# A planned order for the attention stage, seven products for the third group's queries and keys, and rotated rows by DMA

## The chip, the cores and the metric

The kernel runs on one core of one Trainium2 chip. The metric is the device time of one execution in microseconds (us). The core has five instruction streams that run beside each other and meet at semaphores: PE (TensorE, matmuls), DVE (VectorE), ACT (ScalarE), POOL (GpSimd) and SP (SyncE, which here issues nearly all loads from memory). PSUM holds the matmuls' sums in banks of 512 columns.

## What is computed

Two layers on 512 tokens of width 1024. Each layer has a mixer and a gated FFN; scale, shift and gate vectors come from a conditioning vector `c`. Layer 0's mixer is a recurrent one (hgrn), layer 1's is the attention that is changed here: three groups with windows and dilations, mixed by their log sums.

```python
DILATED_GROUPS = ((128, 1), (512, 4), (2048, 16))

def dilated_attention_mixer(u, cos, sin, w_in, w_out):
    proj = (u @ w_in).reshape(B, S, N_GROUPS, 3, ATT_HEADS, ATT_HEAD_DIM)
    for gi, (window, dilation) in enumerate(DILATED_GROUPS):
        q = apply_partial_rope(proj[:, :, gi, 0], cos, sin) * scale
        k = apply_partial_rope(proj[:, :, gi, 1], cos, sin)
        v = proj[:, :, gi, 2]
        o_g, lse_g = dilated_group_attention(q, k, v, window, dilation)
    wts = jax.nn.softmax(jnp.stack(lses, axis=0), axis=0)
    o = jnp.einsum('gbsh,gbshd->bshd', wts, jnp.stack(outs, axis=0))
    return o.reshape(B, S, D_MODEL) @ w_out

def reference(...):
    cond = jax.nn.silu(c)
    for layer in range(2):
        mod = cond @ ada_w[layer] + ada_b[layer]
        sh1, sc1, g1, sh2, sc2, g2 = jnp.split(mod, 6, axis=-1)
        u = rms_norm(h, norm_g[layer, 0]) * (1.0 + sc1) + sh1
        y = hgrn2_mixer(u, ...) if layer == 0 else dilated_attention_mixer(u, ...)
        h = h + (1.0 + g1) * rms_norm(y, norm_g[layer, 1])
        u = rms_norm(h, norm_g[layer, 2]) * (1.0 + sc2) + sh2
        h = h + (1.0 + g2) * rms_norm(swiglu_ffn(u, ...), norm_g[layer, 3])
```

The rotation (`apply_partial_rope`) touches the first 32 of a head's 128 dimensions. In the text "vector (l, v)" is the v-th of the six vectors of layer l, counted from 0: (1,4) is the second scale of layer 1.

## The kernel before

**Products in three parts.** Every float32 operand is cut into hi (a cast to the reduced type fp32r) and lo (the remainder), and every product is hi·hi + hi·lo + lo·hi on PE (`three`, L438 to L440 for most of them).

**The stream of weights.** All weights come through `Stream`, in one list of items. SP loads an item (1 MB, `_load`, L59 to L68) into one of two raw tiles; ACT casts hi (L88), DVE subtracts for lo (L89), and a raw tile is free for the next load when lo is done. There are three pairs of hi and lo tiles. `take()` hands out the next weight and casts up to two weights ahead of it (`ahead = parts - 1`), `take(0)` casts no further than the one that it hands out. Items of the conditioning vectors ("ada", `ada_chunk`) stand in the same list, put between weights by `weave`: a load of 1 MB, four sums on DVE (L257, L259), after every second one a reduction over partitions on POOL (L261), and then small sums with the identity on DVE (L271, L275).

**Seven products.** Some products are done as a block scheme: the weight is taken in quarters of 512 columns, and seven products of quarter sums replace eight. The first FFN's `seven_products` (matmuls at L853) does this with 84 matmuls of 128x256 where 96 would be needed; `seven_values` does it for the values of groups 1 and 2 of the attention.

**The attention stage.** `order` lists units: for each of eight heads and three groups one unit "qk" (queries and keys, a weight of 1 MB: 2 x 8 x 3 = 48 matmuls of 128x512 by `block`), and units "v" for values. After the two halves of a unit `qk_evac` (L1704, L1705) has ACT copy 32 rows to be rotated, and all 128 rows, out of PSUM; `turn_pair` (L1712 to L1715 on DVE) rotates the rows, and four copies on ACT (L1720, L1722) put them back. The rest of a head (scores, exponentials, weights of the groups, scaling of the probabilities in `merge_r` and `merge_n` on DVE (L1798, L1805), transposes `flip` with their copies on DVE (L1817) and ACT (L1815), sums with V) is given to `Fillers`, which runs it a fixed number of half units later. There is no planner: outside hand-ordered stretches (`manual_schedule`, which keeps the code's order on PE, ACT, DVE and POOL) the framework's scheduler sets the order of each engine.

**The seam.** Behind the last unit comes `mixer_out`, the product with `attn_w_out` (four weights), in the code's own order. It asks for its first weight with `take(0)` at kt = 0 and for the second at kt = 4; between its products stand the rest of heads 6 and 7 (`tail`). By then the stage's own `take()` calls have cast two weights ahead. `cut(kt)` makes hi and lo of the attention's output (`oh`, `ol`).

Of the kernel before, what the change touches and what calls it, by code (L numbers as in the profile page):

```python
# [1 line left out]

# [13 lines left out]
P = 128  # L16
# [21 lines left out]
class Stream:  # L38
# [73 lines left out]
    def whole(self):  # L112

        assert self.items[self.done][0] in WHOLE
        self.fill()
        self.done += 1
        return self.raw.pop(self.done - 1)
# [10 lines left out]
    def take(self, ahead=None):  # L128
        ahead = self.parts - 1 if ahead is None else ahead
        k = min(self.taken + ahead, len(self.wpos) - 1)  # L130
        stop = next((i for i in range(self.done, len(self.items)) if self.items[i][0] in WHOLE), len(self.items))
        self.process_to(min(self.wpos[k] + 1, stop))
        if k == len(self.wpos) - 1:
            self.process_to(stop)
        self.taken += 1
        return self.ready.pop(0)

# [21 lines left out]
def block_kernel(tc, x, c, positions, ada_w, ada_b, norm_g, hgrn_w_in, lower, hgrn_norm_g, hgrn_w_out,  # L159
# [8 lines left out]
    with ExitStack() as ctx:  # L168
# [95 lines left out]
        def ada_item(l, v, hf, kq):  # L264
            src = ada_w[l, kq * 512:(kq + 1) * 512, v * D + hf * 512:v * D + (hf + 1) * 512]
            return ("ada", src.rearrange("(k p) n -> p k n", p=P), ada_chunk(l, v, hf, kq))
# [43 lines left out]
        def fin_item(l, v, hf):  # L310
            if v not in (2, 5):
                return ("do", None, col_fin(l, v, hf))
# [3 lines left out]
            return ("rows", (b, n), row_fin(l, v, hf))  # L316
# [62 lines left out]
        items += weave(f0b[:9], ada_seq((1, 1), (1, 0)), 0, 0.9) + f0b[9:]  # L379
# [31 lines left out]
        late = ada_seq((1, 2), (1, 4), (1, 3))  # L411
# [3 lines left out]
        woven(late[:8], 1.5)  # L415
# [4 lines left out]
        woven(late[8:], 1.3)  # L420
# [16 lines left out]
        def three(ps, ah, al, bh, bl, start, stop):  # L437
            pe.matmul(ps, ah, bh, start=start, stop=False)  # L438
            pe.matmul(ps, ah, bl, start=False, stop=False)  # L439
            pe.matmul(ps, al, bh, start=False, stop=stop)  # L440
# [942 lines left out]
        def seven_values(dsts, apart, th, tl):  # L1383


            C = lambda raw, c: V4(raw)[:, :, c * 256:c * 256 + 256]
            G = lambda t, o: V4(t[:, o * 1024:(o + 1) * 1024])
            u_of = lambda r, c: lambda kt, n: [a[:, r * 4 + kt, c * 256 + n * P:c * 256 + (n + 1) * P] for a in apart]
            t_of = lambda i: lambda kt, n: [a[:, i, kt, n * P:(n + 1) * P] for a in (th, tl)]
            raws, tiles = {}, {}  # L1390

            def cut(i, tile, o, k, c):
                hi, lo = tiles[i, tile]
                src = C(raws[i][k], c)
                act.copy(G(hi, o), src)
                dve.tensor_sub(G(lo, o), src, G(hi, o).bitcast(F32))

            def place(i, tile):
                tiles[i, tile] = st.part_tiles(V0)

            def prepare(i, step):
                if i >= len(dsts):
                    return
                if step == 0:
                    raws[i] = [st.whole(), st.whole()]
                    place(i, 0)
                    cut(i, 0, 0, 0, 0)
                    cut(i, 0, 1, 1, 1)
                elif step == 1:
                    place(i, 1)  # L1410
                    cut(i, 1, 0, 1, 0)
                    a, b = raws[i]
                    dve.tensor_add(C(b, 1), C(b, 1), C(a, 1))
                    dve.tensor_add(C(a, 1), C(a, 1), C(a, 0))
                    dve.tensor_add(C(a, 0), C(a, 0), C(b, 1))
                    dve.tensor_add(C(b, 0), C(b, 0), C(a, 0))
                    cut(i, 1, 1, 0, 0)
                elif step == 2:
                    place(i, 2)
                    cut(i, 2, 1, 0, 1)  # L1420
                    st.fill(1)
                    cut(i, 2, 0, 1, 1)
                else:
                    place(i, 3)
                    cut(i, 3, 0, 1, 0)
                    raws.pop(i)
                    st.fill()

            def run(ps, i, tile, o, us):
                hi, lo = tiles[i, tile]  # L1430
                for n in range(2):
                    for kt in range(4):
                        w = slice(o * 1024 + kt * 256, o * 1024 + (kt + 1) * 256)
                        three(ps[:, n * 256:(n + 1) * 256], *us(kt, n), hi[:, w], lo[:, w], kt == 0, kt == 3)

            H2 = lambda a: a.rearrange("p (n c) -> p n c", n=2)
            for step in range(3):
                prepare(0, step)
            for i, dst in enumerate(dsts):
                X, Y, Z, U = (dst[:, t:t + 2, c:c + 256] for c in (0, 256) for t in (0, 2))  # L1440
                m1 = bank("mm")
                run(m1, i, 0, 0, u_of(0, 0))
                act.copy(X, H2(m1))
                m4 = bank("a")
                run(m4, i, 0, 1, t_of(2))
                prepare(i, 3)
                m2 = bank("mm")
                run(m2, i, 1, 0, u_of(1, 0))
                m6 = bank("mm")
                run(m6, i, 1, 1, t_of(3))  # L1450
                dve.tensor_add(Y, X, H2(m6))
                dve.tensor_add(X, X, H2(m2))
                prepare(i + 1, 0)
                m5 = bank("mm")
                run(m5, i, 2, 0, t_of(0))
                m7 = bank("mm")
                run(m7, i, 2, 1, t_of(1))
                dve.scalar_tensor_tensor(Z, Y, -1.0, H2(m7), op0=OP.mult, op1=OP.subtract)
                dve.tensor_add(Y, Y, H2(m5))
                dve.tensor_sub(U, Z, H2(m5))  # L1460
                dve.tensor_sub(Z, Z, H2(m4))
                prepare(i + 1, 1)
                m3 = bank("mm")
                run(m3, i, 3, 0, u_of(1, 1))
                dve.tensor_add(Y, Y, H2(m3))
                prepare(i + 1, 2)

# [383 lines left out]
        fl.n = 0  # L1851
        for kind, g, i in order:
            if kind == "v":
                if g == 1:

                    for fn in fl.at.pop(fl.n, []):
                        fn()
                    seven_values(V[1:], apart, th, tl)
                    if i:
                        act.dma_start(V[0], v_away)  # L1860
                continue
            if g == 0:
                heads[i] = {}
                n = fl.n
                fl.add(n + 3, lambda i=i: scores(i, 0))
                fl.add(n + 5, lambda i=i: scores(i, 1))
                fl.add(n + 7, lambda i=i: scores(i, 2))
                fl.add(n + 9, lambda i=i: (merge_r(i), merge_n(i)))
# [50 lines left out]
```

## Time and profile before

| | us |
|---|---|
| median of 3 runs | 1510.66 (1510.45 to 1511.49) |
| profiled execution | 1511.44 |
| its span, first to last instruction | 1509.4 |
| PE busy | 1493.7 (99%) |
| first FFN, sixteen seven-product units | 383.40 to 537.31 |
| first FFN, down products | from 537.31 |
| attention: units of queries and keys, values, heads | 704.36 to 1107.39 |
| `mixer_out` of the attention | from 1107.39 |

Busy time alone doesn't say what bounds a stage; it is read from the waits of PE in that stage and from what released them. In rows of a timeline the first number is the start and the second the duration; a matmul's duration is its latency, and the pace is the distance between starts. In rows of groups the numbers behind the bar are busy time and mean nanoseconds, then the idle time of the engine before them and what ended it.

### The profile page before, as it was taken

The page shows a single profiled execution, that of the slowest core. Times are in us where ns is not written, and L with a number is a line of the kernel's source. Part 1 is how long each engine was busy: PE and PEld are TensorE (multiplying, and loading weights), DVE is VectorE, ACT ScalarE, POOL GpSimd, SP SyncE. Part 2 cuts the span into 40 slices and gives each one's busy share as a digit, 9 for nine tenths or more (in the row PEclk, how much of TensorE's full clock was granted, in tenths as well). Part 3 has the DMA queues.
Part 4 walks back from the last instruction along what each step waited for, and adds up shares of the span by engine and source line. Part 5 has one row for each costly group of instructions (what it writes and reads, how often), then busy time and mean ns, then how long its engine had stood idle before and what let it go on. Part 6 is the DMA issues. An engine that isn't in the chain of part 4 may idle for free. (4 is left out here: it accounts for less than half of the span.)

```text
span 1509.4 us, 23492 instructions
## 1 busy us (share of the span) xinstructions
PE 1493.7 (99%) x9231; PEld 1309.7 (87%) x9231; DVE 1040.2 (69%) x1807; ACT 746.6 (49%) x1321; POOL 199.0 (13%) x174
## 2 busy tenths in 40 slices
PE   8999999999999999999999999999999999999998
PEld 6777888898999988888988888988888899999886
DVE  4587768486888876577668766686466978887533
ACT  4443433362555542376546666356655555555231
POOL 1011211030111101040001110011002211110100
PEclk9999999999999999999999999999999999999999
DMA  9553444125333356424166540365213333334531
GB/s 309 166 183 126 156 152 168 56 85 167 101 109 107 107 200 213 155 108 141 57 183 191 151 120 29 123 185 141 84 52 117 100 97 112 112 112 141 199 108 56
DMA packets 206942, 199.14 MB, mean 132 GB/s; under 512 B 6840, under 2 KB 164720, under 8 KB 206576
## 3 DMA queue, kind: packets, MB, share of 16 engines
q1 hardware_dynamic: 203856, 190.87, 40.3%
q10 hardware_dynamic: 1952, 6.65, 1.2%
q8 instruction: 72, 1.18, 0.3%
q0 software_dynamic: 1024, 0.13, 0.2%
q14 instruction: 38, 0.31, 0.1%
HBM read 192.31 MB, written 5.31 MB: 131 GB/s over the span
## 5 line engine op out<-in xcount | busy, mean ns | idle before, releaser
L88 ACT CAST hi<-raw 128x2048 fp32r<-128x2048 f32 x68 | 129.7, 1907 | 199.1 <-DMA raw<-in_ffn_w_out_dram 60.8
L89 DVE TENSOR_TENSOR lo<-raw,hi 128x2048 fp32r<-128x2048 f32 x68 | 161.5, 2377 | 96.2 <-ACT hi L88 96.2
L438 PE MATMUL ps_mm<-apart,hi 128*128 128x512 f32 x384 | 151.4, 394 | 0.0
L439 PE MATMUL ps_mm<-apart,hi 128*128 128x512 f32 x384 | 151.2, 394 | 0.0
L440 PE MATMUL ps_mm<-apart,lo 128*128 128x512 f32 x384 | 150.6, 393 | 0.0
L438 PE MATMUL ps_mm<-uh,hi 128*128 128x512 f32 (+1 forms) x400 | 146.3, 366 | 0.0
L439 PE MATMUL ps_mm<-ul,hi 128*128 128x512 f32 (+1 forms) x400 | 144.3, 361 | 1.0 <-DVE ul L538 1.0
L440 PE MATMUL ps_mm<-uh,lo 128*128 128x512 f32 (+1 forms) x400 | 144.6, 361 | 0.0
L438 PE MATMUL ps_mm<-hi,oh 128*128 128x512 f32 x240 | 94.0, 392 | 0.0
L853 PE MATMUL ps_mm<-th,hiq 128*128 128x256 f32 x340 | 93.9, 276 | 0.0
L853 PE MATMUL ps_mm<-tl,hiq 128*128 128x256 f32 x340 | 93.9, 276 | 0.0
L853 PE MATMUL ps_mm<-th,loq 128*128 128x256 f32 x340 | 93.9, 276 | 0.0
L439 PE MATMUL ps_mm<-lo,oh 128*128 128x512 f32 x240 | 93.4, 389 | 0.0
L438 PEld LDWEIGHTS ps_mm<-uh,hi 128*128 128x128 f32 x400 | 75.5, 189 | 19.7 <-issue 8.4
L844 DVE TENSOR_TENSOR loq<-raw,hiq 128x1024 fp32r<-128x1024 f32 x68 | 80.2, 1221 | 16.8 <-ACT hiq L840 16.8
L439 PEld LDWEIGHTS ps_mm<-ul,hi 128*128 128x128 f32 x400 | 75.6, 189 | 12.1 <-DVE ul L538 1.4
L440 PEld LDWEIGHTS ps_mm<-uh,lo 128*128 128x128 f32 x400 | 75.5, 189 | 11.4
L824 POOL TENSOR_TENSOR raw<-raw 128x512 f32<-128x512 f32 x34 | 45.1, 1328 | 305.1 <-DVE spare L820 131.3
L440 PEld LDWEIGHTS ps_mm<-apart,lo 128*128 128x128 f32 x384 | 72.2, 188 | 14.5
L439 PEld LDWEIGHTS ps_mm<-apart,hi 128*128 128x128 f32 x384 | 72.2, 188 | 14.2
L438 PEld LDWEIGHTS ps_mm<-apart,hi 128*128 128x128 f32 x384 | 72.2, 188 | 14.1
L259 DVE SCALAR_TENSOR_TENSOR shared<-raw,cond,shared 128x512 f32<-128x512 f32 x98 | 73.2, 747 | 12.9 <-DMA raw<-in_ada_w_dram 11.9
(440 smaller groups left out, 4183.5 us busy)
## 6 DMA issues: line engine op xcount, KB each, us to landing
raw<-in_ada_w_dram SPq DMA_DIRECT2D x40, 1024.0 KB, 5.1
raw<-in_ffn_w_in_dram SPq DMA_DIRECT2D x136, 256.0 KB, 3.6
raw<-in_attn_w_in_dram SPq DMA_DIRECT2D x48, 512.0 KB, 5.1
raw<-in_ffn_w_out_dram SPq DMA_DIRECT2D x22, 1024.0 KB, 4.9
raw<-in_hgrn_w_in_dram SPq DMA_DIRECT2D x12, 1024.0 KB, 5.4
raw<-in_attn_w_in_dram SPq DMA_DIRECT2D x12, 1024.0 KB, 4.9
raw<-in_ffn_w_in_dram SPq DMA_DIRECT2D x10, 1024.0 KB, 5.0
first<-in_ada_w_dram SPq DMA_DIRECT2D x14, 512.0 KB, 7.9
```

Of the source, the lines that this page charges most:

```text
L88: self.nc.scalar.copy(hi, t)
L89: self.nc.vector.tensor_sub(lo, t, hi.bitcast(F32))
L259: dve.scalar_tensor_tensor(a, r[:, k], sc, a, op0=OP.mult, op1=OP.add)
L438: pe.matmul(ps, ah, bh, start=start, stop=False)
L439: pe.matmul(ps, ah, bl, start=False, stop=False)
L440: pe.matmul(ps, al, bh, start=False, stop=stop)
L824: pool.tensor_add(r[:, 2], r[:, 2], r[:, 0])
L844: dve.tensor_sub(lo, src, hi.bitcast(F32))
L853: pe.matmul(ps, w[x][:, a], us[kt][y], start=begin and kt + m == 0, stop=kt == 3 and m == 2, skip_group_check=True)
```

## The change

1. **A planner.** A class `Plan` takes the attention stage as tasks (engine, cost, what is read and written) and simulates them: each engine takes, among the tasks that are ready, the one due first; goals come from PE's running clock. The order that results is then written out by hand for PE, ACT, DVE, POOL and SP.
2. **Third group by seven products.** For `g == 2` a "qk" item is loaded in quarters (four transfers of 256 KB), DVE adds quarters (four additions), and seven products of 12 matmuls of 128x256 replace the 48 of 128x512. Sums are accumulated on seeds: ACT copies a finished half bank into the next bank, and the next product adds to it.
3. **Rows by DMA.** For groups 1 and 2 the rotated rows go back by four transfers on SP (32x256 each) instead of four copies on ACT.
4. **Other work.** Scaling of the probabilities goes from DVE to ACT (eight instructions a head), and all copies of flips go to ACT.
5. **Vectors.** (1,4) goes from the attention stage to the down products of the first FFN; (1,2) and (1,3) stay, at other places.
6. **The seam.** The plan ends with the last unit (`heads_end`), and no `take()` with its two weights ahead is called in the stage any more; `mixer_out` itself is as before.

```diff
-        items += weave(f0b[:9], ada_seq((1, 1), (1, 0)), 0, 0.9) + f0b[9:]
+        items += weave(f0b, ada_seq((1, 1), (1, 0), (1, 4)), 0, 0.69)
...
+        by_seven = lambda g: g == 2
         def aqk(g, hd):
-            return ("w", tuple(AW[:, (g * 3 + k) * D + hd * P:(g * 3 + k) * D + (hd + 1) * P].rearrange(
-                "(k p) n -> p k n", p=P) for k in range(2)))
+            w = [AW[:, (g * 3 + k) * D + hd * P:(g * 3 + k) * D + (hd + 1) * P].rearrange("(k p) n -> p k n", p=P) for k in range(2)]
+            return ("quarters", (w[1], w[0])) if by_seven(g) else ("w", tuple(w))
...
-        late = ada_seq((1, 2), (1, 4), (1, 3))
+        late = ada_seq((1, 2), (1, 3))
...
-        woven(late[:8], 1.5)
+        woven(late[:6], 2)
...
-        woven(late[8:], 1.3)
+        woven(late[6:], 2)
+        heads_end = len(items)
...
+            if g:
+                for i, t in enumerate((q, k)):
+                    for n in range(2):
+                        o = (2 * i + n) * 32
+                        COPY(lambda t=t, n=n, o=o: nc.sync.dma_start(t.t[0:32, n * 256:n * 256 + 256], rows.t[o:o + 32]),
+                             [rows(2 * i + n)], [t(n)])
...
+            def products_1():
+                s_["b"] = first, both, u2, u4 = [mm_of() for _ in range(4)]
+                s_["xs"] = xs = slot("xs", 1, [P, 512], mk)
+                run(first, 0, 0, a_of(0, 0), True)
+                ACT(0.36, lambda: act.copy(u2.t[:, lo], first.t[:, lo]), [first()], [u2()], urgent=True)
+                run(both, 0, 1, T3, True)
+                ACT(0.36, lambda: act.copy(xs.t[:, lo], both.t[:, lo]), [both()], [xs(0)])
+                run(u2, 0, 2, t2, False)
+                ACT(0.36, lambda: act.copy(u4.t[:, lo], u2.t[:, lo]), [u2()], [u4()], urgent=True)
...
+                run(first, 1, 3, a_of(1, 0), False)
+                queries(first, 0)
+                run(u4, 1, 0, t1, False)
+                ACT(0.36, lambda: act.copy(xs.t[:, hi], u4.t[:, lo]), [u4()], [xs(1)], urgent=True)
+                run(u2, 1, 2, T4, False)
+                keys(1, 1, both)
+                keys(0, 0, u2)
+                run(u4, 1, 1, a_of(1, 1), False)
+                queries(u4, 1)
+                turned(g, rows, q, k)
...
-            whi, wlo = st.take()
-            pair = []
-            for k in range(2):
-                ps = block(whi, wlo, k * D, P, u=apart)
-                heads[i]["qk"[k], g] = qk_evac(ps, g, k, pair)
-                if k == 1:
-                    turn_pair(g, pair)
-                fl.tick()
...
+        with tc.manual_schedule(engines=ORDERED | {mybir.EngineType.SP}):
+            planned = plan.run()
+        st.done, st.taken = heads_end, st.taken + sum(k == "qk" and not by_seven(g) for k, g, _ in order)
```

In the order of ACT before, near the end of the attention stage, the hi casts of the first and of the second weight of `attn_w_out` (`hi_9829`, `hi_9952`) stand among the evictions of the last units, the second one well ahead of the three cuts `oh` of `mixer_out`:

```order
L88 CAST hi_9829<-raw_9604 128x2048
L1704 ACTIVATE shared<-ps_mm_9771 32x256 x2
L1705 ACTIVATE qk_9796<-ps_mm_9771 128x512
L1772 ACTIVATE h,sR_9707<-h,nR_9708 128x256 x4
L1785 ACTIVATE wE_9903<-wE_9903 128x8
L1720 COPY qk_9758<-shared 32x2x128 x2
L1720 COPY qk_9796<-shared 32x2x128 x2
L1704 ACTIVATE shared<-ps_mm_9835 32x256 x2
L1705 ACTIVATE qk_9860<-ps_mm_9835 128x512
L88 CAST hi_9952<-raw_9731 128x2048
```

In the changed order of ACT the same two casts are `hi_10602` and `hi_10739` (the line is now L89); `ps_mm_10421` is the last product of the last unit:

```order
L2107 ACTIVATE shared<-ps_mm_10421 32x256
L2108 ACTIVATE qk_10315<-ps_mm_10266 128x256
L2108 ACTIVATE qk_10315<-ps_mm_10421 128x256
L570 CAST oh_10583<-oT_6093 128x512
L570 CAST oh_10584<-oT_6094 128x512
L570 CAST oh_10585<-oT_6095 128x512
L89 CAST hi_10602<-raw_10188 128x2048
...
L1836 ACTIVATE wE_10692<-wE_10692 128x8
L1680 DMA h<-h_away 128x1024
L570 CAST oh_10656<-oT_late_6099 128x512
L1836 ACTIVATE wE_10724<-wE_10724 128x8
L89 CAST hi_10739<-raw_10351 128x2048
```

The first cast moved behind the last eviction and the three cuts, the second behind the last exponential of the group weights (`wE`). On PE, the changed order from the last product of the last unit into `mixer_out`:

```order
L2007 MATMUL ps_mm_10421<-apart_6300,loq_10295 128x256
L2372 MATMUL ps_b_10234<-h,V_6105 128x128
...
L2351 MATMUL ps_a_10489<-ident,h 128x128 x3
L2351 MATMUL ps_a_10503<-ident,h 128x128 x4
L574 MATMUL ps_mm_10587<-hi_10602,oh_10583 128x512
L2294 MATMUL ps_a_10569<-qk_10231,qk_10230 128x128 x4
L575 MATMUL ps_mm_10587<-lo_10603,oh_10583 128x512
L576 MATMUL ps_mm_10587<-hi_10602,oT_10593 128x512
```

Eight sums with V and seven transposes stand between the last product and the first matmul that reads `hi_10602`; the scores of head 7's second group now stand between that one and the first that reads `lo_10603`. On SP, the loads in the down products of the first FFN, from the fourth weight on (`in_ffn_w_out` weights, `in_ada_w` vectors), in the changed order:

```order
L69 DMA raw_5117<-in_ffn_w_out_dram 128x2x1024
L69 DMA raw_5179<-in_ada_w_dram 128x4x512
L69 DMA raw_5185<-in_ada_w_dram 128x4x512
L69 DMA raw_5290<-in_ffn_w_out_dram 128x2x1024
L69 DMA raw_5296<-in_ada_w_dram 128x4x512
L69 DMA raw_5302<-in_ffn_w_out_dram 128x2x1024
L69 DMA raw_5375<-in_ada_w_dram 128x4x512
L69 DMA raw_5381<-in_ada_w_dram 128x4x512
L69 DMA raw_5443<-in_ffn_w_out_dram 128x2x1024
L69 DMA raw_5459<-in_ada_w_dram 128x4x512
```

Before, weights and vectors took turns one by one; now two vector loads stand ahead of every second weight.

More of the change, by code (lines that the diff above doesn't have):

```diff
@@ L112, in whole @@
     def whole(self):
-        assert self.items[self.done][0] in WHOLE
+        self.process_to(next(i for i in range(self.done, len(self.items)) if self.items[i][0] in WHOLE))
         self.fill()
@@ L1381, in tok_proj @@
                 done(t, ps)
[L1383 to L1466, printed above, removed]
```

588 lines of the change are left out of this document (561 added, 27 removed).

## The prediction

> **What bounds the kernel now.** I read the page's first part, then the table of windows, then PE's waits. The page's busy times:
>
> ```profile
> span 1509.4 us, 23492 instructions
> PE 1493.7 (99%) x9231; PEld 1309.7 (87%) x9231; DVE 1040.2 (69%) x1807; ACT 746.6 (49%) x1321; POOL 199.0 (13%) x174
> ```
>
> PE is busy for 99% of the span, so the time is what PE has to do plus the few places where it waits. The windows (start:end, length, then busy time and count for PE, PEld, DVE, ACT, POOL, clock, DMA share, GB/s) are the seven-product part of the first FFN, the attention stage that is rewritten, and mixer_out behind it:
>
> ```profile
> 383.40:537.31 153.91, 153.91 (x1346) 153.91 (x1344) 122.51 (x131) 87.56 (x145) 19.68 (x16) 1.00 0.40 117
> 704.36:1107.39 403.03, 401.87 (x2302) 352.11 (x2301) 267.34 (x694) 230.36 (x452) 40.30 (x36) 1.00 0.42 126
> 1107.39:1141.00 33.61, 33.61 (x188) 28.96 (x187) 19.70 (x60) 14.90 (x30) 1.32 (x2) 1.00 0.35 119
> ```
>
> In the attention window PE lacks 1.16 us of 403. Its waits there, all of them (line, releaser, total, times, longest):
>
> ```profile
> PE ps_a L1743 <- ACT qk L1720: 0.6, 1, 0.6
> PE ps_b L1837 <- ACT h L1815: 0.3, 1, 0.3
> PE ps_b L1846 <- ACT h L1815: 0.2, 1, 0.2
> ```
>
> DVE (66%) and ACT (57%) are only cover here. Two things can therefore change the time: the number of PE cycles, and a new wait on PE.
>
> **Part 1: fewer PE cycles.** The first two rows are the ends of 24 plain matmuls of 128x512, the next two the ends of sixteen seven-product units of the FFN, the last two the ends of 24 matmuls of 128x256 in the value products:
>
> ```profile
> 704.36 0.39 PE L438 MATMUL ps_mm<-apart,hi 128*128 128x512 f32 x1
> 709.80 0.39 PE L438 MATMUL ps_mm<-apart,hi 128*128 128x512 f32 x1
> 383.40 0.28 PE L853 MATMUL ps_a<-uh,spare 128*128 128x256 f32 x1
> 537.31 0.40 PE L438 MATMUL ps_mm<-hi,oh 128*128 128x512 f32 x1
> 732.21 0.28 PE L438 MATMUL ps_a<-hiq,uh 128*128 128x256 f32 x1
> 735.06 0.28 PE L439 MATMUL ps_mm<-loq,apart 128*128 128x256 f32 x1
> ```
>
> Plain: 5.44/24 = 0.2267 us each, so a unit of 48 (queries and keys of one group and head) is 10.88 us. Seven products: 153.91/16 = 9.62 us for a unit of 84, of which the new one is a copy in number and shape. Eight heads change their third group: 8 x (9.62 - 10.88) = -10.1 us. Ends: at the value products' pace, 2.85/24 = 0.1188 us, a unit is 9.98 and the gain 7.2; at exactly seven eighths of 10.88 it is 10.9. I take 10.1, since the FFN's chain (one bank after the other, no addition on PE) is the nearest.
>
> **Part 2: what the new units ask of ACT and DVE.** In each unit two sums in PSUM begin on a seed: ACT copies a finished half bank (128x256) into the next bank, and PE comes back to that bank twelve matmuls later, 12 x 0.1145 = 1.37 us. The nearest rows for the copy, and for the casts it can stand behind on ACT (group, busy us and mean ns):
>
> ```profile
> L1443 ACT COPY V<-ps_mm 128x512 f32<-128x512 f32 x4 | 2.4, 589 | 2.7 <-PE ps_mm L440 2.6
> L1395 ACT CAST hiq<-raw 128x1024 fp32r<-128x1024 f32 x28 | 28.7, 1048 | 42.9 <-DMA raw<-in_attn_w_in_dram 9.2 <-PE ps_mm L440 8.7 <-PE ps_mm L439 6.8
> L1798 DVE TENSOR_SCALAR h<-h,wE 128x256 f32<-128x256 f32 x28 | 8.3, 356 | 0.2
> L1722 ACT COPY qk<-shared 32x256 f32<-32x256 f32 x60 | 24.1, 402 | 13.8 <-DVE shared L1715 12.8 <-DVE wZ L1789 0.3
> ```
>
> Half of 512 columns is at most the 589 ns, nearer 0.36; with 0.2 us from PE's end to ACT (E and 1105.13 below) and 0.2 back, 0.6 us are left. A seed whose turn comes just as ACT begins a cast of 1.05 us is 0.45 late. Nothing is queued on PE that could step in. I count two such misses in sixteen, +1.0 (ends 0 and nine misses, +4). The three waits shown go with the order that made them: -1.1 (ends -1.1 and 0).
>
> What else moves is cover. DVE gets four raw sums and four differences more per unit and loses the scaling (eight of 356 ns per head) and its flip copies; ACT gets those and loses the copies of rotated rows (L1722, 402 ns each). ACT goes up by some 30 us, to about 65% of the window, DVE stays; both keep a third. The rows come back as 32 KB transfers on SP instead: four per unit, behind a weight load in the worst case. The page's median landings are
>
> ```profile
> raw<-in_ada_w_dram SPq DMA_DIRECT2D x40, 1024.0 KB, 5.1
> raw<-in_ffn_w_in_dram SPq DMA_DIRECT2D x136, 256.0 KB, 3.6
> ```
>
> so at most 5.1 + 3.6 = 8.7 us, against a unit and more (over 10.9 us) until the scores that read them; I cost them at nothing, and where a load in front waits for a raw tile it is PE that pays what exceeds that unit.
>
> **Part 3: conditioning vector (1,4) moves into the down products of the first FFN.** Four more 1 MB loads (twelve for eight) go among the same eleven weights on the same two raw tiles, each with four sums on DVE, its diagonals (DVE) and reductions (POOL) behind; the attention stage is rid of as many. The sums' group, then the loads now, a weight's remainder between two of them:
>
> ```profile
> L259 DVE SCALAR_TENSOR_TENSOR shared<-raw,cond,shared 128x512 f32<-128x512 f32 x98 | 73.2, 747 | 12.9 <-DMA raw<-in_ada_w_dram 11.9
> 567.25 0.37 SPq L68 DMA_DIRECT2D raw<-in_ffn_w_out_dram  x1
> 574.09 2.29 DVE L89 TENSOR_TENSOR lo<-raw,hi 128x2048 fp32r<-128x2048 f32 x1 [2.76 <-ACT hi L88]
> 576.41 0.37 SPq L68 DMA_DIRECT2D raw<-in_ffn_w_out_dram  x1
> 605.33 9.80 SPq L68 DMA_DIRECT2D raw<-in_ffn_w_out_dram  x3
> SPq L68 <- DVE lo L89: 49.0, 10, 10.1
> ```
>
> A weight's tile comes free 9.16 us after its issue, when the remainder is done, and eight issues (567.25 to 605.33) take 38.08 us, 4.76 each. From weight 3 to weight 10 the change has 16 steps of 4.76 = 76.2 us; PE asks for a weight every 10.88, and seven of these are 76.2. On average it just holds, with no more reserve; a pair of vector loads (eight sums, 8 x 0.75 = 6.0 us of DVE, ahead of the next remainder) before weights 4, 6 and 8 makes those late, and weight 3 starts with about 3 us in hand. By hand I find weights 6 and 8 short by 0.6 to 1.0. I take +1.5 (0 to 4).
>
> **Part 4: attn_w_out is no longer cast ahead.** Before, the stage's own hand-outs cast its first two pieces during the last heads. In the changed order hi of the first stands on ACT behind the last unit's evictions and three cuts, and hi of the second behind the last weights' exponential (L1785). The last products and the turn into mixer_out now:
>
> ```profile
> 1104.93 0.38 PE L1836 MATMUL ps_b<-h,V 128*128 128x128 f32 x2
> 1105.13 0.76 ACT L1704 ACTIVATE shared<-ps_mm 32x256 f32<-32x256 f32 x2 [1.67 <-PE ps_mm L440]
> 1105.91 0.60 ACT L1705 ACTIVATE qk<-ps_mm 128x512 f32<-128x512 f32 x1
> 1106.53 1.66 ACT L434 CAST oh<-oT 128x512 fp32r<-128x512 f32 x3
> 1107.39 0.47 PE L438 MATMUL ps_mm<-hi,oh 128*128 128x512 f32 x1
> 1110.33 1.06 PE L1761 MATMUL ps_a<-qk,qk 128*128 128x128 f32 x8
> 1091.53 1.91 ACT L88 CAST hi<-raw 128x2048 fp32r<-128x2048 f32 x1 [1.14 <-PE ps_mm L439]
> ```
>
> Let E be the end of the last product, 1104.93. PE fills 2.46 us with sums and flips and then needs hi. ACT: 0.20 to start, 0.38 for rows, 0.7 for two half evictions, 1.6 for three cuts, 1.9 for the cast: hi at E + 4.7, a stall of **2.2**. The second matmul needs lo, 2.29 us (the 574.09 row's kind) after hi: E + 7.1, while PE with one matmul and scores of 0.9 us between is there at E + 5.9: **1.2** more. Together +3.4.
>
> The second piece, at kt = 4 (scores of head 7, group 3; PE's need; the exponential; the last scaling):
>
> ```profile
> 1112.79 1.06 PE L1761 MATMUL ps_a<-qk,qk 128*128 128x128 f32 x8
> 1121.85 0.39 PE L438 MATMUL ps_mm<-hi,oh 128*128 128x512 f32 x1
> 1117.88 2.28 DVE L435 TENSOR_TENSOR oT<-oT,oh 128x512 fp32r<-128x512 f32 x3 [2.66 <-ACT oh L434]
> 1123.77 0.21 ACT L1785 ACTIVATE wE<-wE 128x8 f32<-128x8 f32 x1 [2.24 <-DVE wE L1784]
> 1124.89 1.08 DVE L1805 TENSOR_SCALAR h<-h,wE 128x128 f32<-128x128 f32 x4
> ```
>
> From these scores (T) PE needs hi at T + 9.06. The exponential ends at T + 11.19, and this chain starts anew from T however late T is. Cast: T + 13.10, a stall of **4.0**. lo waits for the scaling to end (T + 13.18) and takes 2.29: T + 15.5, PE is at its second matmul at T + 13.3: **2.2**. Together +6.2. Behind these no engine catches up: PE holds the only queue that matters, so both add. Ends for the two places together: 7.3 if the 2.28 us of subtractions (1117.88) leave the chain, 10.8 if two copies of flips (0.6 each) come ahead of a cast.
>
> [...]
>
> **Sum.** -10.1 - 1.1 + 1.0 + 1.5 + 3.4 + 6.2 = +0.9 us. The profiled execution took 1511.44 us (2.04 around its span) and lies 0.78 above the median of 1510.66: 1512.3 for it, **1511.6** as a median. The gain is real and is handed back at the seam.
>
> **Rivals.** *The seam is cheaper (faster).* All low ends: -10.9 - 1.1 + 0 + 0 + 7.3 = -4.7, 1506.0. For it: the eight units' saving rests on a row of the same shape, and the weights' chain may shorten. Against: the order of ACT and DVE is fixed here. Were both pieces in time by some path, -10.1 - 1.1 + 1.0 + 1.5 = -8.7 and 1502.0; the order speaks against it. *Seeds (slower).* ACT at 65% with casts of 1.05 us: if all sixteen seeds are caught, 16 x 0.45 = 7.2 in place of 1.0, 1517.8; it decides from nine misses on, where the total passes +3. For it: each seed has one narrow window; against: the planner marks two of them as urgent. *Loads (slower side).* Part 3 at its end: 1514.1; for it the balance of 76.2 against 76.2, against it 3 us in hand. *Clock (slower).* Early in the trace, where PE has gaps, the clock falls:
>
> ```profile
> 10.00:20.00 10.00, 7.07 (x41) 5.38 (x42) 7.30 (x17) 7.47 (x15) 2.90 (x4) 0.77 1.11 345
> ```
>
> Ten microseconds at 0.77 lose 2.3; after the stall at kt = 4 that gives 1513.9.
>
> **Chances.** A measurement of this kernel tells 0.2%, 3.0 us, from no change: 1507.6 to 1513.7. Forecast 0.42 (own range 1508 to 1514); cheap seam 0.20, both pieces in time 0.04; seeds 0.17; loads or clock 0.17. So faster 0.24, same 0.42, slower 0.34. The range 1505.5 to 1518.5 leaves out the 0.04, the tails of seeds and a little of the cheap seam.
>
> **What would show it.** In the new trace: the window of the attention stage some 11 us shorter, its third groups at 9.6 us per 84; a wait of about 2 us on hi and 1 on lo at mixer_out's first matmuls; about 4 and 2 at kt = 4; short waits on lo among the first FFN's down products. Wrong would be: no idle PE at the seam (then 1502), or waits on seeds spread over all heads (then 1518).

## The result: 1527.95 us, 1.1% slower

Four executions of the changed kernel took 1525.55 to 1532.68 us, median 1527.95; the kernel before took 1510.58 beside them. The ratio is 1.0109, with an interval of 1.0094 to 1.0123. The forecast of no measurable change, and its range up to 1518.5, were wrong. The profiled execution is the longest of the four, 1532.68; its page begins:

```profile
span 1531.0 us, 24376 instructions
PE 1494.6 (98%) x9519; PEld 1323.6 (86%) x9519; DVE 1071.4 (70%) x1832; ACT 772.0 (50%) x1406; POOL 198.3 (13%) x174
```

Two things stand out. PE's busy time did not fall, though it has fewer cycles to do, and the span grew by 21.6 us. The windows of the changed kernel from the first matmul of the units to the end of the last unit's last product, and from there to the FFN's first transposes into a bank b (columns as before; the last three figures of a row are granted clock, DMA share and GB/s):

```profile
708.45:1113.03 404.58, 393.96 (x2568) 359.97 (x2567) 277.35 (x677) 251.21 (x530) 32.71 (x32) 0.99 0.39 115
1113.03:1173.32 60.29, 51.40 (x256) 43.02 (x255) 31.37 (x77) 26.72 (x54) 4.00 (x7) 0.92 0.32 107
```

The reader is to see three figures in each: length, PE's busy time, clock. PE is idle for 10.6 us in the first and 8.9 us in the second, and the clock is below 1.00 in both. Cut at the same instructions, the two profiled executions compare as follows:

| stretch (profiled executions, us) | before | after | difference | predicted |
|---|---|---|---|---|
| start to the first FFN's down products | 537.31 | 538.56 | +1.2 | 0 |
| down products to the first unit | 167.05 | 169.89 | +2.8 | +1.5 |
| units, values and heads | 400.57 | 404.58 | +4.0 | -10.2 |
| seam: last product to the FFN's transposes | 46.51 | 60.29 | +13.8 | +9.6 |
| rest | 357.96 | 357.68 | -0.3 | 0 |

The first row is not the change's: the code there is the same, and over all profiled executions of this study that stretch took 535.1 to 538.6. PE's waits in the two stretches that matter:

```profile
PE ps_mm L2007 <- ACT ps_mm L2092: 9.3, 6, 4.5
PE ps_mm L574 <- ACT hi L89: 6.2, 2, 3.8
PE ps_a L2294 <- ACT h L2359: 2.2, 2, 1.3
PE ps_mm L575 <- DVE lo L90: 1.9, 1, 1.9
```

L574 and L575 are the seam, as forecast; of the two waits at L2294 (scores that wait for a copy of a flip) one of 1.3 us lies in the stage and one of 0.8 at the seam. L2092 is the first seed copy of a third-group unit: six of the eight were late, one by 4.5 us. That one, in the timelines of PE, ACT and DVE:

```profile
1018.96 0.28 PE L2007 MATMUL ps_mm<-uh,loq 128*128 128x256 f32 x1
1023.70 0.58 PE L2007 MATMUL ps_mm<-uh,hiq 128*128 128x256 f32 x1 [4.46 <-ACT ps_mm L2092]
```

```profile
1018.21 0.77 ACT L2159 ACTIVATE shared<-ps_mm 32x256 f32<-32x256 f32 x2
1023.17 0.21 ACT L2322 ACTIVATE wE<-wE 128x8 f32<-128x8 f32 x1 [4.19 <-DVE wE L2321]
1023.28 0.37 ACT L2092 COPY ps_mm<-ps_mm 128x256 f32<-128x256 f32 x1
```

```profile
1022.70 0.16 DVE L2319 TENSOR_TENSOR wM<-sN,oN 128x4 f32<-128x4 f32 x1 [6.79 <-DMA oN<-scr]
```

Read backwards: PE waits for the seed (L2092); the seed had its data long before, but on ACT it stands right behind the exponential of the N weights (L2322); that one waits for DVE, and DVE for `oN`, a 4 KB transfer that brings the row sums back from memory. ACT did nothing for 4.2 us with the seed next in line. In seven of the eight heads the planned order has this exponential directly ahead of the seed, and five of the six late seeds are among them (7.8 of the 9.3 us). These are the rows of ACT's order for the third head:

```order
L2322 ACTIVATE wE703_7591<-wE703_7591 128x8
L2092 COPY ps_mm726_7847<-ps_mm716_7727 128x256
L2138 CAST hiq23_7866<-raw113_7818 128x1024 x2
```

The sixth late seed, the first head's, has no exponential ahead of it. It waited for a sum of the values on DVE and cost PE 1.4 us:

```profile
776.96 0.36 ACT L2092 COPY ps_mm<-ps_mm 128x256 f32<-128x256 f32 x1 [2.50 <-DVE V L2247]
```

The transfers in the air during the stall of 4.5 us (KB each, median us to landing):

```profile
raw<-in_attn_w_in_dram SPq DMA_DIRECT2D x4, 512.0 KB, 5.7
scr<-sR POOLq DMA_DIRECT2D x1, 4.0 KB, 3.3
oN<-scr POOLq DMA_DIRECT2D x1, 4.0 KB, 5.9
```

The planner had put down 2.2 us for each landing. Beside 2 MB of weights the sums' two trips took 3.3 and 5.9. Over the seven heads the way back (`oN`) took 2.3 to 2.4 us in five, 4.0 and 5.9 in two, and the write ahead of it 1.9 to 4.1.

Behind that stall the array ran at half clock. Three windows of the changed kernel, during the stall, behind it, and after that:

```profile
1019.20:1023.70 4.50, 0.04 (x1) 0.00 (x1) 0.96 (x8) 0.48 (x2) 1.57 (x1) 0.99 0.61 144
1023.80:1027.00 3.20, 3.20 (x15) 3.20 (x16) 2.97 (x17) 2.17 (x7) 0.00 (x0) 0.50 0.02 5
1027.20:1032.00 4.80, 4.80 (x45) 4.80 (x44) 2.70 (x10) 4.26 (x11) 0.00 (x0) 1.00 0.11 29
```

In the second PE is busy throughout at clock 0.50, with 15 matmuls in 3.2 us where the third has 45 in 4.8. This is the main reason why PE's busy time did not fall.

### The profile page after: what moved, and what is told of

It reads as the page before. It is cut to its first block, busy times and chain, and to the rows that moved or that the text cites. A ratio compares the mean times of both kernels' runs of the same rounds, so it can differ in the third digit from the quotient of the medians.

```text
span 1531.0 us, 24376 instructions
## 1 busy us (share of the span) xinstructions
PE 1494.6 (98%) x9519; PEld 1323.6 (86%) x9519; DVE 1071.4 (70%) x1832; ACT 772.0 (50%) x1406; POOL 198.3 (13%) x174
## 5 line engine op out<-in xcount | busy, mean ns | idle before, releaser
L2007 PE MATMUL ps_mm<-apart,hiq 128*128 128x512 f32 (+1 forms) x672 | 187.0, 365 | 0.0
L89 ACT CAST hi<-raw 128x2048 fp32r<-128x2048 f32 x45 | 85.9, 1908 | 140.5 <-DMA raw<-in_ffn_w_out_dram 65.7
L574 PE MATMUL ps_mm<-uh,hi 128*128 128x512 f32 (+1 forms) x400 | 146.3, 366 | 0.0
L575 PE MATMUL ps_mm<-ul,hi 128*128 128x512 f32 (+1 forms) x400 | 144.3, 361 | 1.1 <-DVE ul L674 1.1
L90 DVE TENSOR_TENSOR lo<-raw,hi 128x2048 fp32r<-128x2048 f32 x45 | 107.5, 2392 | 52.5 <-ACT hi L89 52.3
L2007 PEld LDWEIGHTS ps_mm<-apart,hiq 128*128 128x128 f32 x672 | 118.0, 189 | 17.3
L2007 PE MATMUL ps_mm<-apart,loq 128*128 128x512 f32 (+1 forms) x336 | 120.5, 359 | 0.0
L574 PE MATMUL ps_mm<-hi,oh 128*128 128x512 f32 x240 | 95.1, 397 | 6.2 <-ACT hi L89 6.2
L575 PE MATMUL ps_mm<-lo,oh 128*128 128x512 f32 x240 | 95.2, 397 | 2.7 <-DVE lo L90 2.7
L574 PEld LDWEIGHTS ps_mm<-uh,hi 128*128 128x128 f32 x400 | 75.5, 189 | 19.8 <-issue 8.4
L575 PEld LDWEIGHTS ps_mm<-ul,hi 128*128 128x128 f32 x400 | 75.6, 189 | 12.1 <-DVE ul L674 1.5
L976 ACT CAST hiq<-raw 128x1024 fp32r<-128x1024 f32 x68 | 68.0, 1048 | 17.5 <-DVE raw L964 16.6
L2007 PEld LDWEIGHTS ps_mm<-apart,loq 128*128 128x128 f32 x336 | 63.2, 188 | 9.7
L576 PE MATMUL ps_mm<-hi,ol 128*128 128x512 f32 x176 | 68.5, 389 | 0.0
L989 PEld LDWEIGHTS ps_mm<-th,loq 128*128 128x128 f32 x340 | 63.8, 188 | 0.0
```

Source lines behind the costliest of these rows:

```text
L89: self.nc.scalar.copy(hi, t)
L90: self.nc.vector.tensor_sub(lo, t, hi.bitcast(F32))
L574: pe.matmul(ps, ah, bh, start=start, stop=False, skip_group_check=part)
L575: pe.matmul(ps, ah, bl, start=False, stop=False, skip_group_check=part)
L576: pe.matmul(ps, al, bh, start=False, stop=stop, skip_group_check=part)
L976: act.copy(hi, src)
```

## The experiments

Each run has 4 to 12 executions, and each median is set against the kernel before in the same set of runs (1512.63, 1513.24 and 1513.72 us in the three sets; it was 1510.58 beside the change's first runs). Some expectations give a time that was counted from the first runs, so what compares is the distance to the kernel before: 1514, 1515, 1525 and 1524 are 3.4, 4.4, 14.4 and 13.4 above it. The stretches are those of the table above, from one profiled execution each.

| run | median - before | to first unit | units and heads | seam |
|---|---|---|---|---|
| before | 0 | 167.05 | 400.57 | 46.51 |
| c1_after, the change again | +16.8 | 172.38 | 402.83 | 60.52 |
| b1_seam, before with the seam | +12.9 | 167.05 | 402.69 | 60.82 |
| s1_seam, attn_w_out cast in the plan | +10.2 | 172.05 | 407.24 | 48.37 |
| s2_late5, later landing | +5.8 | 171.12 | 393.02 | 59.55 |
| s3_vec, vector (1,4) back | +16.0 | 167.05 | 402.52 | 60.32 |
| s4_plain, no seven products | +15.1 | 172.37 | 400.41 | 60.28 |
| s5_both, s1 and s2 | -5.0 | 173.05 | 392.55 | 48.58 |
| s6_all, s5 and vector back | -5.6 | 167.04 | 396.74 | 48.58 |
| s7_spread, s5, loads spread | +2.1 | 177.63 | 393.05 | 48.57 |
| s8_rows, s5, rows by ACT | -4.5 | 170.24 | 392.85 | 51.34 |
| s9_two, s5, two groups | -0.9 | 172.46 | 394.61 | 52.01 |
| s10_plan, s5, no seven products | -1.9 | 170.41 | 398.07 | 46.54 |

### The change again

> The changed kernel itself again, on the chip of the runs beside it, so that they can be compared with it. 15 to 18 us above the kernel before.

1530.06 against 1513.24, 16.8 above, as expected. PE waited for its seeds for 7.5 us in all, once for 5.4, against 9.3 in the first profile: the same order does not cost the same each time.

### The seam alone, in the old kernel

```diff
-        fl.n = 0
+        fl.n = units = 0
...
-            whi, wlo = st.take()
+            left = sum(k == "qk" for k, _, _ in order) - units
+            units += 1
+            whi, wlo = st.take(min(2, left - 1))
```

> The kernel before with nothing of the change but its seam: the last two units of the attention stage hand out their weight with less cast ahead, so that hi of attn_w_out's first weight stands behind the three cuts and hi of the second behind the last exponential. Theory (stalls of 2.3 and 1 at kt = 0, 3.8 and 1.9 at kt = 4, and each of the longer ones followed by 3.4 us at half clock, up to three such stretches at 1.6 us lost each): 12 to 14 us above the kernel before, clock 0.5 behind the stalls. Rival (only the stalls count): 9 above. Rival (the seam's price belongs to the planned order and not to the missing cast): under 4 above.

1526.11 against 1513.24, ratio 1.0093 (1.0078 to 1.0107): +12.9. PE's waits at the seam, and the window of the seam, from this kernel:

```profile
PE ps_mm L438 <- ACT hi L88: 3.8, 1, 3.8
PE ps_mm L439 <- DVE lo L89: 3.4, 2, 1.8
PE ps_a L1761 <- DVE h L1817: 1.0, 1, 1.0
```

```profile
1105.27:1166.09 60.82, 52.47 (x255) 43.58 (x254) 31.64 (x78) 27.53 (x54) 3.25 (x6) 0.89 0.31 104
```

The waits sum to 8.2 us and the window is 14.3 longer than before. The other 6 us are growth of PE's busy time: it worked 10.2 us of the window at half clock, which makes 5.1 of them. At kt = 0 the waits fall otherwise than in the change (1.0 for scores and 1.8 for lo), at kt = 4 they are 3.8 and 1.6. With nothing of the plan, the missing cast alone costs what it costs in the changed kernel. Both rivals fall.

### The seam repaired in the changed kernel

```diff
+        AHEAD = 2
+
+        def out_weight():
+            raw = next_weights()
...
+            p = plan.place("hl", 3, make)
+            for n in range(2):
+                two = slice(n * 1024, n * 1024 + 1024)
+                ACT(1.0, lambda two=two: act.copy(p.t[0][:, two], raw.t[:, two]), [raw()], [p("h", n)], goal=clock[0])
+                DVE(1.15, lambda two=two: dve.tensor_sub(p.t[1][:, two], raw.t[:, two], p.t[0][:, two].bitcast(F32)),
+                    [raw(), p("h", n)], [p("l", n)], goal=clock[0])
+            done_with_raw()
+        for _ in range(AHEAD):
+            out_weight()
         with tc.manual_schedule(engines=ORDERED | {mybir.EngineType.SP}):
...
```

> The changed kernel with the first two weights of attn_w_out cast inside the plan, at the end of the attention stage. Theory (the seam costs its stalls and the half clock behind them): 2.4 + 0.8 us at kt = 0 and 3.8 + 1.9 at kt = 4 go, and with them some 5 us of half clock: 1527.9 - 13.8 = about 1514; no wait of PE on hi or lo in mixer_out. Rival 1 (the stalls go but the clock loss is not theirs): 1527.9 - 8.9 = 1519. Rival 2 (the two casts on ACT make seeds of the last heads later): 4 us or more of new waits before mixer_out, above 1518.

1522.87, 10.2 above the kernel before, where the change itself lay 16.8 above on the next set. The seam fell from 60.3 to 48.4 us, 12 of the 13.8. But the stage before it was longer, 407.24, with these waits:

```profile
PE ps_mm L2007 <- ACT ps_mm L2092: 10.8, 5, 4.5
PE ps_a L2294 <- ACT h L2359: 1.3, 1, 1.3
PE ps_mm L2007 <- DVE loq L2184: 1.1, 1, 1.1
PE ps_mm L574 <- ACT qk L2108: 0.7, 1, 0.7
```

Those seeds are the ones late in the change too, ahead of the casts in the order (the longest at 937 and 1025 us). So the seam theory holds by its stretch, and the median shows less of it than expected. The time is that of rival 2, but not by its mechanism: the new waits are not in the last heads. Beside the later landing the repair shows nearly in full: from s2_late5 to s5_both the seam falls from 59.55 to 48.58 us, and the distance to the kernel before by 10.8.

### Seeds: the exponential behind the copy

```diff
-                     [("scr", hd, 1)], late=2.2)
+                     [("scr", hd, 1)], late=5.0)
-            POOL(0.75, ..., [("scr", hd, 1)], [oN()], late=2.2)
+            POOL(0.75, ..., [("scr", hd, 1)], [oN()], late=5.0)
```

The same number is changed for the two other transfers of sums (`scr` of the N group, `oR`).

> The changed kernel with the planner told that the small transfers of sums through memory (scr, oR, oN on POOL) land 5.0 us after issue, not 2.2; in the order that results, the exponential of the N weights stands behind the first seed copy of each third-group unit and no longer right ahead of it. Theory (the seed waits on ACT behind an exponential that waits for oN): the 9.3 us of waits on seeds and some 3.4 us of half clock go: about 1515. Rival (the round trip is needed anyway, and PE then waits at the transposes or sums that read the scaled rows): waits of the same size at those lines, 1525 to 1530.

1518.38, 5.8 above: the largest gain of one edit. On ACT the N exponential now stands behind the seed (the head with the stall of 4.5 us):

```profile
1011.18 0.36 ACT L2092 COPY ps_mm<-ps_mm 128x256 f32<-128x256 f32 x1
1011.48 0.90 ACT L2335 ACTIVATE h<-h,wE 128x256 f32<-128x256 f32 x2
1012.28 0.19 ACT L2322 ACTIVATE wE<-wE 128x8 f32<-128x8 f32 x1
```

and of the waits on seeds 0.8 us is left; no wait of that size came at another line, the seam's stayed:

```profile
PE ps_mm L574 <- ACT hi L89: 6.2, 2, 3.8
PE ps_mm L2007 <- DVE loq L2184: 1.7, 1, 1.7
PE ps_mm L575 <- DVE lo L90: 1.6, 1, 1.6
PE ps_a L2294 <- ACT h L2359: 1.3, 2, 0.8
PE ps_mm L2007 <- ACT ps_mm L2092: 0.8, 1, 0.8
```

The stage took 393.02 us, 11.6 less than in the change and 7.6 less than before. The longer landing time changes the planned order as a whole and not that one place; the waits on seeds are what it was expected to remove, and what went.

### The conditioning vector back

```diff
-        items += weave(f0b, ada_seq((1, 1), (1, 0), (1, 4)), 0, 0.69)
+        items += weave(f0b[:9], ada_seq((1, 1), (1, 0)), 0, 0.9) + f0b[9:]
...
-        late = ada_seq((1, 2), (1, 3))
+        late = ada_seq((1, 2), (1, 4), (1, 3))
...
-        woven(late[:6], 2)
+        woven(late[:8], 1.5)
...
-        woven(late[6:], 2)
+        woven(late[8:], 1.3)
```

> The changed kernel with conditioning vector (1,4) back in the attention stage, woven as before the change. Theory (the move costs the first FFN 2.8 us up to the first attention unit): 1525, with the way from the down products to the first unit of attention 2.8 us shorter and the two waits on lo gone. Rival (four more loads and sixteen sums in the attention stage cost the plan more than that): 1529 or more.

1528.62, 16.0 above, no gain that can be told from the change's own 16.8. The way to the first unit fell to 167.05, exactly the old value, so the move's price there is shown: 2.8 to 6.0 us over the profiles that have it as in the change. With the repairs (below, s6_all) the four loads cost the attention stage 4.2 us instead. The move is a wash.

### No seven products

```diff
-        by_seven = lambda g: g == 2
+        by_seven = lambda g: False
```

> The changed kernel with no group by seven products: the third group is a plain unit of 48 matmuls again, planned order and all else as changed. Theory (seven products save 8.9 us of PE and cost 9.3 of waits on seeds and 3.4 of half clock): 1527.9 + 8.9 - 12.7 = about 1524. Rival (the planner's order makes PE wait whatever the units are, for the exponential ahead of other copies): waits of 5 us or more stay in the stage and the time is 1530 or more.

1527.72, 15.1 above, so in the change as it stands the seven products are worth nothing: the stage took 400.41 us here and 404.58 and 402.83 with them. No seed waits are left by construction; 2.4 us of waits of another kind (L2294) remain, far under the rival's 5. Counted from the kernel before, the theory had 13.4 and the run 15.1; the way to the first unit was 172.37 us in this profile, 2.5 more than in the change's.

### Both repairs, and both with the vector back

> The changed kernel with both repairs, attn_w_out cast in the plan and the longer landing time for the sums' small transfers. Theory (seeds and seam are two prices that add): the run with the later landing lay 5.8 above the kernel before and still has the whole seam, 9.6 of waits and 3 to 5 of half clock; so 4 to 8 below the kernel before. Rival (the casts in the last heads cost seeds): 0 to 4 above.

> The run with both repairs, and conditioning vector (1,4) back in the attention stage. Theory (the move cost 2.8 to 5.3 us between the first FFN's down products and the first attention unit, in four profiles): another 3 to 5 below the run with both, 8 to 12 below the kernel before. Rival (four more loads in the plan cost it as much, as the run with the vector alone, 0.5 us below or above, suggests): equal to the run with both within 1.5 us.

1508.21 and 1507.60 against 1513.24, ratios 0.9966 (0.9954 to 0.9978) and 0.9965 (0.9952 to 0.9978): both beat the kernel before, by 5.0 and 5.6 us. By stretches the two prices add, as the theory had it: stage and seam are 12.0 and 11.7 shorter than in the change, against 11.6 in s2_late5 and 11.9 in s1_seam. By medians the two together gain more (21.8 us) than one by one (6.6 and 11.0), because the stage of s1_seam was longer. s6_all is not faster than s5_both: its way to the first unit is 6.0 shorter and its stage 4.2 longer, with seeds late again (3.0 us against 0.5) and half clock behind a wait of 2.1 us for a value weight, which is 1.9 in s5_both and has none behind it. The window of s5_both's stage, clock 1.00 again:

```profile
708.22:1100.77 392.55, 389.72 (x2568) 356.63 (x2567) 279.97 (x680) 252.35 (x527) 32.78 (x32) 1.00 0.42 120
```

### The planned order without seven products, repaired

> The run with both repairs without any seven products: the planned order, rows by DMA and moved vector alone. Theory (the planned order by itself is worth nothing beyond the 1.1 us of waits, the vector costs 3 to 5): 2 to 4 above the kernel before, so seven products are worth 7 to 9 us by the difference to the run with both. Rival (the planned order is itself a gain): below the kernel before.

1511.85, 1.9 below, ratio 0.9987 (0.9977 to 0.9998): not the 2 to 4 above of the theory. That the planned order is itself a gain, as the rival has it, is barely shown, since the interval ends next to 1. The stage is 2.5 us shorter than before, but it has also lost the vector's four loads; the way to the first unit is 3.4 longer. From the down products to the seam's end PE waits only in the first FFN:

```profile
PE ps_mm L655 <- DVE xn L649: 1.5, 2, 0.8
PE ps_mm L575 <- DVE lo L90: 1.0, 2, 0.7
```

```profile
708.32:1106.39 398.07, 398.07 (x2279) 350.12 (x2278) 242.61 (x609) 235.66 (x480) 33.88 (x33) 1.00 0.42 122
```

PE is busy here for 398.07 us of 398.07, in s5_both for 389.72 of 392.55. So eight units by seven products save 8.35 us of PE, and 2.8 of that goes in waits of the stage and 2.0 at the seam (48.58 against 46.54).

### Rows by ACT again

```diff
-                        COPY(lambda t=t, n=n, o=o: nc.sync.dma_start(t.t[0:32, n * 256:n * 256 + 256], rows.t[o:o + 32]),
-                             [rows(2 * i + n)], [t(n)])
+                        ACT(0.4, lambda t=t, n=n, o=o: act.copy(t.t[0:32, n * 256:n * 256 + 256], rows.t[o:o + 32]),
+                            [rows(2 * i + n)], [t(n)])
```

> The run with both repairs, with the rotated rows of groups 1 and 2 put back by four copies on ACT per unit, as before the change, in place of four transfers on SP. Theory (rows by DMA cost and gain nothing on PE, the scores stand a unit later): 5 below the kernel before, as the run with both, within 1.5 us. Rival (the transfers stand in SP's queue ahead of weights and make these late): 2 us or more faster than the run with both. Rival (ACT has no room for 64 more copies of 0.4 us): seeds late again, 3 us or more slower than it.

1509.22, 4.5 below the kernel before: no difference to s5_both that this study can tell. Stage 392.85 against 392.55. The seam is 2.8 longer in this profile, by a wait of 2.2 us for an eviction on ACT (L2108) and half clock behind it, and the way to the first unit 2.8 shorter. Rows by DMA are neither gain nor loss in the repaired kernel.

### Vector loads spread

```diff
-        items += weave(f0b, ada_seq((1, 1), (1, 0), (1, 4)), 0, 0.69)
+        items += weave(f0b, ada_seq((1, 1), (1, 0), (1, 4)), 0, 0.9)
```

> The run with both repairs, with the twelve vector loads of the first FFN spread one to a weight (every 0.9 weights) instead of bunched two before every second weight (0.69). Theory (a pair of vector loads makes the next weight late; on average the two raw tiles just hold): the waits on lo and hi among the down products (3.2 us in that run's profile) go, and the way from the down products to the first attention unit falls from 173.0 to 168 to 170 us: 3 us below the run with both, about 8 below the kernel before. Rival (the load is too much however it is spread): same waits at the last weights, equal to the run with both within 1 us.

1515.85, 2.1 above: a miss of both theory and rival. The waits on lo and hi went, as expected, but the loads now end with the stage, and the norm behind the FFN waits:

```profile
PE ps_mm L655 <- DVE xn L649: 8.6, 2, 8.2
```

```profile
646.50 0.68 DVE L619 TENSOR_TENSOR yg<-ps_a,gate 128x512 f32<-128x512 f32 x1
651.24 1.41 DVE L635 SCALAR_TENSOR_TENSOR h<-yg,rr,h 128x512 f32<-128x512 f32 x2 [3.99 <-POOL rr L625]
```

DVE had the statistics that POOL's small step (`rr`) needs at about 646.5, and got `rr` 4 us later than that; POOL had closed the last vector's reduction at 643.5. Why `rr` took these 4 us was not settled. What the run shows is that loads that end with the stage came out worse: PE waited 8.6 us here, with 6.8 us of half clock behind, where in s5_both with its bunched loads it waited 2.8 on lo and 1.7 on the norm. Whether the late `rr` comes from the vector work is open.

### Two groups by seven products

```diff
-        by_seven = lambda g: g == 2
+        by_seven = lambda g: g >= 1
```

> The run with both repairs, with queries and keys of the second group by seven products too. If a unit by seven products saves 1.0 us and its seeds find ACT free: eight units more, 8 us below the run with both, 13 below the kernel before. If cover runs out (each such unit takes two pairs of hi and lo tiles of three, more sums on DVE and more copies on ACT): new waits on seeds or hi of 8 us or more, equal to or above the run with both.

1512.82, ratio 0.9992 (0.9982 to 1.0003): not told from the kernel before, and 4 us worse than one group against it. The largest waits of this kernel's attention stage and seam:

```profile
PE ps_mm L574 <- ACT qk L2108: 3.8, 1, 3.8
PE ps_a L2269 <- ACT qk L2034: 3.0, 4, 2.3
```

The time is the one that was expected if cover runs out, but the waits are others than those named: seeds cost 2.1 us in all, and the large ones are for evictions and rotated rows that ACT had still to copy, and half clock followed the longest of each.

## Why the prediction was wrong, by its own steps

**Part 1, fewer cycles: right, a little large.** -10.1 was forecast between -7.2 and -10.9; 8.35 us of PE time were saved where no half clock spoils the reading (s10_plan against s5_both).

**Part 2, the seeds: the step that failed.** The prediction saw that a seed has 0.6 us in hand (its 0.2 us from ACT back to PE was an estimate; behind the copy that ended at 1023.65 PE began 0.05 us later), and then priced a late one by the length of the longest instruction that ACT may be in the middle of, a cast of 1.05 us: "0.45 late", two misses, +1.0, at most +4. But ACT, in its written order, was held up by an instruction that *waited*, too. The exponential ahead of the seed is 0.2 us long, and it waited up to 4.2 us for sums that had to come back from memory. PE's waits on seeds were 9.3 us, 7.8 of them behind that exponential, and half clock behind two of them took 3.4 more (two stretches of 1.7): 12.7 where 1.0 stood. A wait of 1.3 at L2294 in the stage comes on top. The rival of late seeds had the place right, but by the same wrong cause, a cast. The pieces were there to be seen: the exponential stood directly ahead of the seed in the changed order, and the row that the prediction itself quoted for the seam (1123.77, idle 2.24 us for DVE) shows the same instruction waiting before. In the order that puts the exponential behind the copy the waits on seeds fell to 0.8 us (s2_late5), which is the test of this cause.

**Part 2, the rest: right.** Rows by DMA cost nothing (s8_rows). The old waits of 1.1 us went; with plain units the stage was 2.5 us shorter than before (s10_plan), for which the vector's move may account in part.

**Part 3, the vector: right in kind, low in size.** +1.5 forecast, with 4 as the upper end; 2.8 measured in the first profile, 3 to 6 in others, three of which (c1_after, s1_seam, s9_two) have half clock behind a gap of 1.8 us among the down products. The prediction looked for late weights; the norm behind the stage was late as well:

```profile
PE ps_mm L655 <- DVE xn L649: 1.2, 2, 0.8
PE ps_mm L575 <- DVE lo L90: 0.8, 2, 0.4
```

These are PE's waits of the changed kernel between the down products and the first unit.

**Part 4, the seam: waits right, price too low.** Forecast 2.2 and 1.2 at kt = 0, measured 2.39 and 0.81 (the latter at the scores); forecast 4.0 and 2.2 at kt = 4, measured 3.78 and 1.91. That is 9.6 against 8.9. The stretch grew by 13.8. The missing 4.9 are growth of PE's busy time: it worked 8.3 us of this stretch at half clock, which makes 4.1 of them.

**The clock rival was right and came on top of the forecast.** It was given 2.3 us once, with a chance of 0.17 that it shares with late loads. It struck behind two seeds and twice at the seam, some 8 us in all. The sum took PE at full clock behind every stall, though the prediction had a lower clock among its rivals (0.77 in ten microseconds early in the trace).

Put together, for the profiled executions: +10.6 and +8.9 of waits, +3.4 and +4.9 of half clock, +2.8 in the first FFN, +1.2 that isn't the change's, -0.3 in the rest, and -10.0 for cycles and old waits make +21.5 (rounded), where the spans differ by 21.6. The -10.0 is no measurement of its own: it is what is left of the stage's +4.0 behind 10.6 and 3.4. The nearest independent figure is 8.35 + 1.16 = 9.5. The profiled execution is also the longest of the four; the medians differ by 17.4, and where a typical execution saves the other 4 us no profile shows.

## What to carry to other kernels

Where an order is fixed per engine, ask of each instruction that PE waits for not how long its neighbours take but what the one directly ahead of it waits for; a short instruction that depends on a trip through memory must not stand ahead of a copy that PE needs. A planner is as good as its longest latency: over all profiles here the trip back of the sums (`oN`) had a median of 2.3 us where next to no other bytes moved and of 4.7 us where 150 GB/s or more did, and a plan that puts down the quiet time puts things into the wrong place. When a stage is rewritten, look at what its old calls did for the stage behind it; here two casts that nobody asked for by name were worth 13 us (b1_seam).

## What the hardware showed that was not expected

In these traces PE's stalls were charged twice, but not all of them. In the windows of a quarter microsecond around the stalls of all runs, half-clock stretches last 3.4 us or a multiple of it (in the changed kernel's clock record, between 100 and 1490 us, three of 3.41 and one of 6.83), and 3.4 us cost 1.5 to 1.7 us of PE work where PE is busy in them. Whether one came went by the length of the gap (gaps in a stretch that is at half clock already are left out):

| gap of PE, us | followed by half clock |
|---|---|
| 1.0 to 1.7 | 0 of 21 |
| 1.8 to 1.9 | 4 of 7 |
| 2.0 to 2.7 | 10 of 10 |
| 3.2 to 8.2 | 12 of 13 |

The one of 3.2 us that went free, from s3_vec (window of the gap, then the 7 us behind it at clock 1.00):

```profile
1053.80:1057.00 3.20, 0.04 (x1) 0.04 (x1) 1.56 (x4) 3.15 (x9) 0.10 (x1) 1.00 0.05 1
1057.00:1064.00 7.00, 7.00 (x60) 7.00 (x61) 5.42 (x27) 6.11 (x17) 0.00 (x0) 1.00 0.62 167
```

So the length of the gap did not settle it alone. Within each trace the changes of clock lie a whole number of 3.413 us apart, and 3.413 is also the shortest half-clock stretch in the clock record. Cut on that grid, the 14 traces have 5659 windows at full clock between 100 and 1490 us. The 26 windows that were followed by half clock had 1.65 us or more without PE work, the other 5633 had 1.66 us or less; the gap of 3.2 us lies on the grid as 1.66 and 1.60. In the changed kernel's trace alone, the four that were followed by half clock had 2.15 to 3.41 us without PE work, the other 398 had 1.44 us or less. Of the windows at half clock, those with 0.60 us or more of idle PE were followed by another at half clock (12 windows), those with 0.55 us or less by full clock (26). These are counts; no run was made to test what sets the clock.
